# Attention in a two-layer hybrid trunk: score and value products of the two array halves issued in turns

## The chip, the cores and the metric

The kernel runs on one core of a Trainium2 chip. A core has a TensorE array of 128 rows by 128 columns for matrix products (PE in the profile; its weight loads are PEld), VectorE (DVE), ScalarE (ACT), GpSimd (POOL) and SyncE (SP), which here only starts DMAs. They work at the same time, each through its own queue of instructions in order, and wait for each other through semaphores. Operands lie in the on-chip memory SBUF; matrix products land in the accumulator memory PSUM. Data comes from the device memory by DMA.

The metric is the device time of one execution, in microseconds (us); less is better.

## The reference

The reference is two layers of a trunk on 256 tokens by 1024 channels. A layer mixes a gated delta rule (8 heads) with a sliding-window attention (16 query heads of 64 channels, 2 key and value heads, window 128, a learned sink for each head), projects both, merges them with gates, and ends in a gated feed-forward part. The change touches the attention alone. Its core:

```python
def swa_sink_attention(q, k, v, sinks):
    # q (B,T,16,64), k and v (B,T,2,64); blocks of 128 queries, each with its own block of keys and the one before
...
    s = jnp.einsum('bnqhgd,bnkhd->bnhgqk', qb, kb) * (D ** -0.5)
    rel = qi + SWA_BLOCK - kj
    mask = (rel >= 0) & (rel < WINDOW) & (blk * SWA_BLOCK + kj >= SWA_BLOCK)
    s = jnp.where(mask[None, :, None, None], s, -jnp.inf)
...
    m = jnp.maximum(jnp.max(s, axis=-1, keepdims=True), sink)
    p = jnp.exp(s - m)
    denom = jnp.sum(p, axis=-1, keepdims=True) + jnp.exp(sink - m)
    o = jnp.einsum('bnqhgk,bnkhd->bnqhgd', p / denom, vb)
```

The 256 tokens are two blocks of 128. The first block sees its own keys alone. A query of the second block sees the keys of its own block up to itself, and those of the first block that lie after its place: 128 keys in all, so one square of 128 by 128 holds all scores of a head, the upper triangle from the block before and the lower one from its own.

## The kernel before

**The time is that of the weights' products.** Every layer multiplies the normalized input with some 130 weight tiles. A weight tile comes by DMA on SP's queue into a pool of six buffers (`raw`, line 170), ScalarE rounds it to the TensorE's fast format (`wH`, L177), VectorE takes what the rounding lost (`wL`, L178), and TensorE adds three products for each block of 128 rows into the tile `acc`: rounded weights by rounded input (L193), by the input's rest (L194), rest of the weights by rounded input (L195). The pool also takes the tiles `wada` of the conditioning, which VectorE multiplies and sums (L231); a free buffer is what starts the next DMA.

**Order.** A scheduler puts the instructions of each engine in order by priority. The delta rule and attention are issued at a high priority (`chain()`), in the order of the list `CHAIN` (L28): in layer 0 "p s i 00 v 01 10 11", in layer 1 "p s i 00 10 01 11 v", where "p", "s", "i" and "v" are parts of the delta rule and two digits are one call `attention(tb, kv)`: the block of queries, and the key and value head. The gates' projections (`gate`, L192 to L195) fill TensorE between them. After the chain the projection of the attention's output (`sH`, `sL`; L956) is issued, which needs all four calls.

**One call of `attention`** works on the eight query heads of one key head. They lie in pairs: four pairs of heads, and in each pair the first head has its 64 channels on partitions 0 to 63 and the second on partitions 64 to 127 (`hfs`). So a score product (64 channels deep) uses one half of the array's rows: head 0 of a pair the upper, head 1 the lower. The four products of the first heads go into one PSUM tile, `ps_cur0`, those of the second heads into `ps_cur1` (L816), and in the second block of queries the products with the earlier keys into `ps_prv0` and `ps_prv1` (L825). The loops name the two halves in turns, but nothing holds the scheduler to that. The products are float32, and each is two instructions in the profile.

All these tiles, the transposes and the value products take their PSUM from one pool of two buffers (`pat`, L116): a tile waits until the last reader of the tile two before it is done.

Then each half `i` goes through the softmax by itself: in the first block L820 adds the mask; in the second L828 copies the scores on ScalarE and L829 puts the earlier keys' scores over them where the mask says so. L836 takes the maximum (VectorE), L845 the exponentials (ScalarE, four instructions), L851 scales by the reciprocal of the sum (ScalarE, four instructions), L854 transposes on TensorE into `ps_pT`. In the first block ScalarE copies the transposed probabilities to `pc` (L858) and one value product follows (L859). In the second VectorE writes two masked copies, `pc` and `pp` (L862, L863), and two value products follow (L864, L865), one with the values of each block. A value product has all 128 rows and 64 columns of the array: half 0 of the heads uses the first 64 columns and writes partitions 0 to 63 of the tile `ps_o`, half 1 the others. The value products of half 0 stand ahead of the transposes of half 1. At the end L867 rounds `ps_o` into `sH` on ScalarE, and L868 writes the rest, `sL`, on VectorE.

The SBUF tiles `s0`, `s1`, `pc` and `pp` share one tag of three buffers (`at2`, L304).

## Time and profile before

| what | value |
|---|---|
| timed runs, median of 3 | 1102.69 us (1102.17 to 1106.59) |
| the profiled execution's own time | 1078.32 us |
| its span (first to last instruction) | 1076.5 us |
| granted TensorE clock, mean | 0.997 |
| DMA, mean over the span | 196 GB/s |
| attention and what fills it, layer 0 | 195.5 to 298.1 us of the span |
| the same, layer 1 | 724.2 to 811.8 us |

The terms of the prediction are differences inside the span. The profiled execution lies 1.8 us above its span and 24.4 us below the median of the timed runs, so a difference is carried over to the median as it is. Rows of the trace are given by the line of the kernel that issued them; `x8` counts instructions, and "[0.78 <-DVE pc L862]" behind a row is the time for which the engine stood idle ahead of it, and who ended it.

### The profile page before, as it was taken

The page shows a single profiled execution, that of the slowest core. Times are in us where ns is not written, and L with a number is a line of the kernel's source. Part 1 is how long each engine was busy: PE and PEld are TensorE (multiplying, and loading weights), DVE is VectorE, ACT ScalarE, POOL GpSimd, SP SyncE. Part 2 cuts the span into 40 slices and gives each one's busy share as a digit, 9 for nine tenths or more (in the row PEclk, how much of TensorE's full clock was granted, in tenths as well). Part 3 has the DMA queues.
Part 4 walks back from the last instruction along what each step waited for, and adds up shares of the span by engine and source line. Part 5 has one row for each costly group of instructions (what it writes and reads, how often), then busy time and mean ns, then how long its engine had stood idle before and what let it go on. Part 6 is the DMA issues. An engine that isn't in the chain of part 4 may idle for free.

```text
span 1076.5 us, 23351 instructions
## 1 busy us (share of the span) xinstructions
PE 1038.8 (96%) x9248; PEld 985.9 (92%) x9248; DVE 846.0 (79%) x1891; ACT 648.3 (60%) x1325; POOL 4.0 (0%) x8
## 2 busy tenths in 40 slices
PE   3899989999999999999999999999999999999998
PEld 1799989978799999999999999997879999999998
DVE  6999976967768899988886999788456879777643
ACT  5388755677545675554445897658674457555432
POOL 0000000000000000000000000000000000000000
PEclk9999999999999999999999999999999999999999
DMA  9864565464555578888976545563015555555561
GB/s 361 323 204 156 193 239 168 154 209 138 170 203 178 175 235 290 284 271 274 333 267 188 174 156 199 196 198 117 23 58 179 193 178 177 179 186 179 179 202 36
DMA packets 60013, 210.48 MB, mean 196 GB/s; under 512 B 6784, under 2 KB 7808, under 8 KB 59904
## 3 DMA queue, kind: packets, MB, share of 16 engines
q1 hardware_dynamic: 59616, 208.72, 58.6%
q8 instruction: 72, 1.18, 0.4%
q10 hardware_dynamic: 288, 0.28, 0.1%
q14 instruction: 37, 0.30, 0.1%
HBM read 207.92 MB, written 1.05 MB: 194 GB/s over the span
## 4 chain that ended last, share of the span: by engine, by line
PE 79%; DVE 10%; ACT 6%; issue 3%; DMA 2%; SPq 0%; DVEq 0%; ACTq 0%
PE acc L193 21%; PE acc L195 21%; PE acc L194 21%; DVE wL L178 3%; ACT wH L177 2%; DVE early L231 2%; DMA raw<-wada 1%; PE ps_kk L607 1%; PE ps_cur L816 1%; PE pa L466 1%; PE pa L467 1%; PE pa L465 1%; DVE kq L553 1%; DVE raw L231 1%; PE ps_o L864 1%
## 5 line engine op out<-in xcount | busy, mean ns | idle before, releaser
L177 ACT CAST wH<-raw 128x1024 fp32r<-128x1024 f32 (+2 forms) x302 | 308.6, 1026 | 243.5 <-PE acc L194 193.8
L178 DVE TENSOR_TENSOR wL<-raw,wH 128x1024 fp32r<-128x1024 f32 (+2 forms) x302 | 360.2, 1195 | 90.9 <-ACT wH L177 87.6
L193 PE MATMUL acc<-hH,wH 128*128 128x256 f32 x1376 | 396.4, 288 | 0.0
L195 PE MATMUL acc<-hH,wL 128*128 128x256 f32 x1376 | 395.3, 287 | 0.1
L194 PE MATMUL acc<-hL,wH 128*128 128x256 f32 x1376 | 393.3, 286 | 0.0
L193 PEld LDWEIGHTS acc<-hH,wH 128*128 128x128 f32 x1376 | 264.1, 192 | 3.3 <-issue 1.8
L194 PEld LDWEIGHTS acc<-hL,wH 128*128 128x128 f32 x1376 | 263.9, 192 | 2.0 <-issue 1.6
L195 PEld LDWEIGHTS acc<-hH,wL 128*128 128x128 f32 x1376 | 263.9, 192 | 1.8 <-issue 0.8
L231 DVE SCALAR_TENSOR_TENSOR raw<-raw,cact 128x1024 f32<-128x1024 f32 x80 | 97.4, 1220 | 20.5 <-DMA raw<-wada 20.3
L195 PE MATMUL acc<-g_b,wL 128*128 128x256 f32 x224 | 63.5, 283 | 0.0
L193 PE MATMUL acc<-g_b,wH 128*128 128x256 f32 x224 | 63.5, 283 | 0.0
L194 PE MATMUL acc<-g_b,wH 128*128 128x256 f32 x224 | 63.4, 283 | 0.0
L553 DVE SCALAR_TENSOR_TENSOR kq<-cr,pt,kq 128x255 f32<-128x255 f32 (+2 forms) x96 | 45.7, 477 | 7.6 <-ACT kq L551 7.4
L193 PEld LDWEIGHTS acc<-g_b,wH 128*128 128x128 f32 x224 | 43.0, 192 | 0.0
L195 PEld LDWEIGHTS acc<-g_b,wL 128*128 128x128 f32 x224 | 42.9, 192 | 0.0
L194 PEld LDWEIGHTS acc<-g_b,wH 128*128 128x128 f32 x224 | 42.9, 191 | 0.0
L1015 DVE SCALAR_TENSOR_TENSOR g<-acc,pt,g 128x255 f32<-128x255 f32 x80 | 38.2, 478 | 0.9
L193 PE MATMUL acc<-sH,wH 128*128 128x256 f32 x128 | 36.2, 285 | 0.7 <-ACT sH L867 0.7
L194 PE MATMUL acc<-mL,wH 128*128 128x256 f32 x128 | 36.4, 285 | 0.0
L194 PE MATMUL acc<-sL,wH 128*128 128x256 f32 x128 | 36.2, 284 | 0.1
L195 PE MATMUL acc<-mH,wL 128*128 128x256 f32 x128 | 36.2, 283 | 0.0
L193 PE MATMUL acc<-mH,wH 128*128 128x256 f32 x128 | 36.2, 283 | 0.0
(335 smaller groups left out, 2004.3 us busy)
## 6 DMA issues: line engine op xcount, KB each, us to landing
raw<-wbig SPq DMA_DIRECT2D x232, 512.0 KB, 3.8
raw<-wada SPq DMA_DIRECT2D x80, 512.0 KB, 4.3
raw<-wdn SPq DMA_DIRECT2D x32, 512.0 KB, 4.2
raw<-wsa SPq DMA_DIRECT2D x24, 432.0 KB, 6.5
early<-wada SPq DMA_DIRECT2D x16, 512.0 KB, 9.1
raw<-wdn SPq DMA_DIRECT2D x16, 384.0 KB, 3.6
x<-xT SPq DMA_DIRECT2D x4, 256.0 KB, 5.5
out<-x SPq DMA_DIRECT2D x8, 128.0 KB, 2.5
```

Of the source, the lines that this page charges most:

```text
L177: A.copy(h, raw)
L178: V.tensor_tensor(lo, raw, h.bitcast(F32), ALU.subtract)
L193: PE.matmul(o, wh, ah, start=first, stop=False)
L194: PE.matmul(o, wh, al, start=False, stop=False)
L195: PE.matmul(o, wl, ah, start=False, stop=last)
L231: return V.scalar_tensor_tensor(raw, raw, 1.0, cact, op0=ALU.mult, op1=ALU.mult, accum_out=modp[l][:, f:f + 1])
L465: PE.matmul(o, hh[:, kt, sl], wh[:, k4], start=kt == 0, stop=False)
L466: PE.matmul(o, hh[:, kt, sl], wl[:, k4], start=False, stop=False)
L467: PE.matmul(o, hl[:, kt, sl], wh[:, k4], start=False, stop=kt == KT - 1)
L553: V.scalar_tensor_tensor(dst[:, sft:], cr[:, :T - sft], w_[:, 3 - sft:4 - sft], dst[:, sft:], op0=ALU.mult, op1=ALU.add)
L607: PE.matmul(pk_, t[:, 0, cs_], t[:, :, cs_], start=True, stop=True)
L1015: V.scalar_tensor_tensor(g[:, sft:], pa_[:, :T - sft], fw[:, i, 2 - sft:3 - sft], g[:, sft:], op0=ALU.mult, op1=ALU.add)
```

## The change

In the scores, a helper `scores` issues the eight products of a tile pair and ties each to the one before (`after`, which holds the order on the engine and adds no semaphore). So they stand in turns: first head, second head, of each pair. In the second block of queries the ScalarE copies of the current scores now stand ahead of the earlier keys' products in the program.

The transposed probabilities of both halves of the heads (`pc`, and `pp` in the second block) are kept until both are there. Then the value products are issued, again tied in turns: half 1, half 0 with the queries' own block, then, in the second block, half 1, half 0 with the earlier block. The PSUM tile `ps_o` is taken after the transposes of both halves and not before. The tag `at2` has six buffers in place of three. Each product, copy and mask is still made once.

```diff
--- before.py
+++ after.py
@@ -302,7 +302,7 @@
         return wk.tile([P] + list(shape), F32, name=name, tag="d2", bufs=3)
 
     def at2(name, shape=(4, P)):
-        return wk.tile([P] + list(shape), F32, name=name, tag="at2", bufs=3)
+        return wk.tile([P] + list(shape), F32, name=name, tag="at2", bufs=6)
 
     ssq = {}
 
@@ -808,27 +808,34 @@
             A.copy(kT[:, :, ts], pk)
 
         def attention(tb, kv):
+
+
             ts = slice(tb * P, tb * P + P)
             hfs = (slice(0, 64), slice(64, 128))
-            pcur = [pat([4, P], name=f"ps_cur{i}") for i in range(2)]
-            for j in range(4):
-                for i in range(2):
-                    PE.matmul(pcur[i][:, j], qT[hfs[i], kv * 4 + j, ts], kT[hfs[i], kv, ts], start=True, stop=True)
+
+            def scores(name, keys):
+                p2 = [pat([4, P], name=f"{name}{i}") for i in range(2)]
+                last = None
+                for j in range(4):
+                    for i in range(2):
+                        m = PE.matmul(p2[i][:, j], qT[hfs[i], kv * 4 + j, ts], kT[hfs[i], kv, keys],
+                                      start=True, stop=True)
+                        last = after(m, last) if last else m
+                return p2
+
+            pcur = scores("ps_cur", ts)
             s_ = [at2(f"s{i}") for i in range(2)]
             if tb == 0:
                 for i in range(2):
                     V.scalar_tensor_tensor(s_[i], bc(C("triu1"), 1, 4), NEG, pcur[i], op0=ALU.mult, op1=ALU.add)
             else:
-                pprv = [pat([4, P], name=f"ps_prv{i}") for i in range(2)]
-                for j in range(4):
-                    for i in range(2):
-                        PE.matmul(pprv[i][:, j], qT[hfs[i], kv * 4 + j, ts], kT[hfs[i], kv, 0:P],
-                                  start=True, stop=True)
                 for i in range(2):
                     A.copy(s_[i], pcur[i])
+                pprv = scores("ps_prv", slice(0, P))
+                for i in range(2):
                     V.copy_predicated(s_[i], bc(C("triu1"), 1, 4).bitcast(I32), pprv[i])
-            po = pat([4, P], name="ps_o")
             vs = slice(kv * 64, kv * 64 + 64)
+            pcs, pps = [], []
             for i in range(2):
                 s = s_[i]
                 hs = slice(kv * 8 + i, kv * 8 + 8, 2)
@@ -853,16 +860,21 @@
                 for j in range(4):
                     PE.transpose(pt_[:, j], s[:, j], C("ident"))
                 pc = at2("pc")
-                o = po[i * 64:i * 64 + 64]
+                pcs.append(pc)
                 if tb == 0:
                     A.copy(pc, pt_)
-                    PE.matmul(o, vtok[:, 0, vs], pc, start=True, stop=True)
                 else:
                     pp = at2("pp")
+                    pps.append(pp)
                     V.tensor_tensor(pc, pt_, bc(C("triu"), 1, 4), ALU.mult)
                     V.tensor_tensor(pp, pt_, bc(C("tril1"), 1, 4), ALU.mult)
-                    PE.matmul(o, vtok[:, 1, vs], pc, start=True, stop=False)
-                    tc.keep_in_program_order(PE.matmul(o, vtok[:, 0, vs], pp, start=False, stop=True))
+            po = pat([4, P], name="ps_o")
+            last = None
+            for blk, ops in ((tb, pcs),) if tb == 0 else ((1, pcs), (0, pps)):
+                for i in (1, 0):
+                    m = PE.matmul(po[i * 64:i * 64 + 64], vtok[:, blk, vs], ops[i], start=blk == tb,
+                                  stop=ops is pps or tb == 0)
+                    last = after(m, last) if last else m
             ks = slice(kv * 4, kv * 4 + 4)
             A.copy(sH[:, ks, ts], po)
             V.tensor_tensor(sL[:, ks, ts], po, sH[:, ks, ts].bitcast(F32), ALU.subtract)
```

The first place is on TensorE in layer 0, at the end of the call for block 0 and key head 0 and the start of the next one. Before, with `ps_pT_2914` the transposes of half 1, `pc_2892` and `pc_2919` the probabilities of half 0 and half 1, `acc` the filling projection and `ps_y16` a part of the delta rule:

```order
L859 MATMUL ps_o_2867<-pc_2892,vtok_185 64x512
L193 MATMUL acc_3486<-hH_182,wH_3376 128x256
L194 MATMUL acc_3486<-hL_183,wH_3376 128x256
L195 MATMUL acc_3486<-hH_182,wL_3377 128x256
L854 MATMUL ps_pT_2914<-ct_85,s1_2864 128x128 x4
L859 MATMUL ps_o_2867<-pc_2919,vtok_185 64x512
L816 MATMUL ps_cur0_3053<-kT_1104,qT_1103 128x128 x4
L661 MATMUL ps_y16_2632<-ut16_2630,lq_2540 32x32 x32
```

With the change (half 1 is `pc_2917`, half 0 `pc_2891`):

```order
L861 MATMUL ps_pT_2912<-ct_85,s1_2864 128x128 x4
L875 MATMUL ps_o_2919<-pc_2917,vtok_185 64x512
L875 MATMUL ps_o_2919<-pc_2891,vtok_185 64x512
L661 MATMUL ps_y16_2632<-ut16_2630,lq_2540 32x32 x32
L821 MATMUL ps_cur0_3053<-kT_1104,qT_1103 128x128
L193 MATMUL acc_3523<-hH_182,wH_3412 128x256
L194 MATMUL acc_3523<-hL_183,wH_3412 128x256
L195 MATMUL acc_3523<-hH_182,wL_3413 128x256
L193 MATMUL acc_3523<-hH_182,wH_3412 128x256
L667 MATMUL ps_z16_2667<-u32_2625,yt16_2665 32x32 x32
L821 MATMUL ps_cur1_3054<-kT_1104,qT_1103 128x128
L821 MATMUL ps_cur0_3053<-kT_1104,qT_1103 128x128
```

The value product of half 0 has moved behind the transposes of half 1 and stands beside that of half 1. Of the next call's scores the first now stands alone, since the first of `ps_cur1` needs the buffer of the value tile, and the others follow in turns; before, the four of `ps_cur0` stood together and those of `ps_cur1` came later.

The second place is on TensorE in layer 1, at the end of the last call. Before, from the value product of half 1 with its own block (`pc_10288`) to that with the earlier block (`pp_10289`); the `acc_10729` products belong to a gate (`hH`, `hL`):

```order
L864 MATMUL ps_o_10233<-pc_10288,vtok_7394 64x512
L193 MATMUL acc_10729<-hH_7230,wH_10628 128x256
L194 MATMUL acc_10729<-hL_7231,wH_10628 128x256
L195 MATMUL acc_10729<-hH_7230,wL_10629 128x256
L193 MATMUL acc_10729<-hH_7230,wH_10628 128x256
L194 MATMUL acc_10729<-hL_7231,wH_10628 128x256
L865 MATMUL ps_o_10233<-pp_10289,vtok_7394 64x512
L195 MATMUL acc_10729<-hH_7230,wL_10629 128x256
```

Behind these come 27 more products of the gates, and then the first of the `sH` projection. With the change:

```order
L861 MATMUL ps_pT_10280<-ct_85,s1_10218 128x128 x4
L875 MATMUL ps_o_10289<-pc_10285,vtok_7394 64x512
L875 MATMUL ps_o_10289<-pc_10257,vtok_7394 64x512
L875 MATMUL ps_o_10289<-pp_10286,vtok_7394 64x512
L875 MATMUL ps_o_10289<-pp_10258,vtok_7394 64x512
L193 MATMUL acc_10793<-sH_9633,wH_10693 128x256
L194 MATMUL acc_10793<-sL_9634,wH_10693 128x256
```

All four value products stand directly behind the transposes of half 1, and the projection of `sH` directly behind them; the gates' products stand further ahead in the call.

The third place is on VectorE in layer 0, in the last call, around the masks of half 0. Before (`raw` rows are the conditioning's products, `wL_3839` a weight tile, `pc_3264` and `pc_3294` half 0 and half 1):

```order
L862 TENSOR_TENSOR pc_3264<-ps_pT_3259,ct_85 128x512
L863 TENSOR_TENSOR pp_3265<-ps_pT_3259,ct_85 128x512
L848 TENSOR_TENSOR sme_3278<-sme_3278,es_3275 128x4
L849 RECIPROCAL sme_3278<-sme_3278 128x4
L231 SCALAR_TENSOR_TENSOR raw_4009,modp0_100<-raw_4009,cact_87 128x1024
L178 TENSOR_TENSOR wL_3839<-raw_3836,wH_3838 128x1024
L862 TENSOR_TENSOR pc_3294<-ps_pT_3289,ct_85 128x512
L863 TENSOR_TENSOR pp_3295<-ps_pT_3289,ct_85 128x512
```

With the change (`pc_3263` half 0, `pc_3291` half 1):

```order
L231 SCALAR_TENSOR_TENSOR raw_4009,modp0_100<-raw_4009,cact_87 128x1024
L869 TENSOR_TENSOR pc_3263<-ps_pT_3258,ct_85 128x512
L870 TENSOR_TENSOR pp_3264<-ps_pT_3258,ct_85 128x512
L855 TENSOR_TENSOR sme_3275<-sme_3275,es_3272 128x4
L856 RECIPROCAL sme_3275<-sme_3275 128x4
L869 TENSOR_TENSOR pc_3291<-ps_pT_3286,ct_85 128x512
L870 TENSOR_TENSOR pp_3292<-ps_pT_3286,ct_85 128x512
```

The conditioning's product `raw_4009` has moved ahead of the masks of half 0. The weight tile `wL_3839` stands ten rows ahead of it now, behind the maxima of the call, and the DMA that fills `raw_4009` takes the buffer that `wL_3839` frees.

## The prediction

> **What bounds the kernel now.** I read the page first: busy times, then the chain that ended last.
>
> ```profile
> span 1076.5 us, 23351 instructions
> PE 1038.8 (96%) x9248; PEld 985.9 (92%) x9248; DVE 846.0 (79%) x1891; ACT 648.3 (60%) x1325; POOL 4.0 (0%) x8
> PE 79%; DVE 10%; ACT 6%; issue 3%; DMA 2%; SPq 0%; DVEq 0%; ACTq 0%
> ```
>
> TensorE is busy for 96% of the span and carries 79% of the chain, so a microsecond of TensorE work that goes is a microsecond of time, as long as no other engine is late at that place. The next reading is therefore by stage: the windows of the eight attention calls, four of each layer (start:end; length, then busy time of PE, PEld, DVE, ACT and POOL, the clock, the DMA share and GB/s).
>
> ```profile
> 195.50:221.18 25.68, 23.66 (x161) 19.55 (x160) 23.52 (x97) 20.67 (x56) 0.00 (x0) 1.00 0.48 163
> 221.18:246.78 25.60, 25.28 (x478) 21.36 (x477) 14.96 (x35) 17.62 (x49) 0.00 (x0) 1.00 0.54 176
> 246.78:278.05 31.27, 31.20 (x230) 26.34 (x229) 26.24 (x68) 19.82 (x54) 0.00 (x0) 1.00 0.48 157
> 278.05:298.07 20.02, 17.79 (x112) 13.07 (x111) 13.85 (x32) 11.35 (x34) 0.00 (x0) 1.00 0.53 175
> 724.20:746.65 22.45, 19.99 (x138) 16.12 (x138) 21.82 (x97) 19.25 (x54) 0.00 (x0) 1.00 0.32 103
> 746.65:772.00 25.35, 25.07 (x466) 19.54 (x465) 11.61 (x28) 17.14 (x49) 0.00 (x0) 1.00 0.24 74
> 772.00:787.04 15.04, 14.95 (x106) 12.44 (x105) 7.53 (x24) 11.21 (x34) 0.00 (x0) 1.00 0.12 36
> 787.04:811.70 24.66, 24.66 (x179) 20.63 (x179) 15.67 (x37) 16.30 (x46) 0.00 (x0) 1.00 0.21 64
> ```
>
> Three kinds of call are seen. In the first of each layer TensorE stands idle for 2.0 and 2.5 us, while DVE and ACT are busy for over 80% of it: they set the pace. In the last of layer 0 TensorE is idle for 2.2 us. In the other five it is idle for 0.4 us or less: there a saved product shortens the call.
>
> **The scores.** How two halves of the rows stand beside each other is in the timeline of TensorE (start, busy time, line, count):
>
> ```profile
> 197.49 0.49 PE L816 MATMUL ps_cur<-kT,qT 64*128 64x128 f32 x4
> 197.91 0.39 PE L194 MATMUL acc<-hL,wH 128*128 128x256 f32 x1
> 246.78 1.16 PE L816 MATMUL ps_cur<-kT,qT 64*128 64x128 f32 x8
> 247.86 1.16 PE L726 MATMUL ps_KS<-s,kq 128*128 128x128 f32 x8
> 724.21 1.16 PE L816 MATMUL ps_cur<-kT,qT 64*128 64x128 f32 x16
> 725.30 0.39 PE L193 MATMUL acc<-hH,wH 128*128 128x256 f32 x1
> ```
>
> From start to next start, four products (8 instructions) of one half take 1.08 us (246.78 to 247.86); four of each half in turns (16 instructions) take 1.09 us (724.21 to 725.30): the second half costs nothing. One product of each half takes 0.42 us (197.49 to 197.91), so a run with k products of a half takes about 0.42 + (2k - 2) x 0.1115 us: 0.42, 0.64, 0.86, 1.09. By the order before, the scores stand in 20 runs, in all 22.8 us by these prices. The order after has 29 runs: 16 with one product of a half, 3 with two, 3 with three, 7 with four. That is 16 x 0.42 + 3 x 0.64 + 3 x 0.86 + 7 x 1.09 = 18.8 us. **Saved: 4.1 us.** It isn't half, since the second tile of scores waits for the buffer of the value tile before it, so the first score stands alone, and fillers come in between.
>
> **The value products.** Sums over the run (count | busy, mean ns | idle ahead; the 8 rounds of the earlier block's products, L865, are like those of L864), then TensorE's timeline of a lone one (two instructions), and of two that follow on the same columns:
>
> ```profile
> L859 PE MATMUL ps_o<-pc,vtok 128*64 128x512 f32 x16 | 8.6, 618 | 2.8 <-ACT pc L858 2.7
> L864 PE MATMUL ps_o<-pc,vtok 128*64 128x512 f32 x16 | 8.6, 618 | 1.3 <-DVE pc L862 1.3
> ...
> 216.26 1.07 PE L859 MATMUL ps_o<-pc,vtok 128*64 128x512 f32 x2
> 217.26 0.38 PE L193 MATMUL acc<-hH,wH 128*128 128x256 f32 x1
> ...
> 290.76 1.07 PE L864 MATMUL ps_o<-pc,vtok 128*64 128x512 f32 x2 [0.78 <-DVE pc L862]
> 291.67 1.02 PE L865 MATMUL ps_o<-pp,vtok 128*64 128x512 f32 x2
> 292.62 0.72 PE L854 MATMUL ps_pT<-ct,s 128*128 128x128 f32 x4
> ```
>
> A lone product holds TensorE for 1.00 us (216.26 to 217.26), two for 1.86 (290.76 to 292.62). The 24 products, 8 of each line (16 instructions), take some 23.8 us (8 x 1.00 for those of L859 and about 2 x 8 x 0.99 for the others, since many of those stand alone between fillers). If the two halves of the columns run beside each other as those of the rows do, the four calls of the first block need 1.00 us each, and the four of the second 1.86: 11.4 us. **Saved: 12.4 us.** If they run one after the other, it is 1.86 and 3.58 us: 4 x 0.86 + 4 x 1.72 = 10.3 us more. No row of before has two halves of the columns in turns. The nearest rows:
>
> ```profile
> 222.27 0.75 PE L661 MATMUL ps_y<-ut,lq 32*32 32x32 f32 x64
> 222.95 0.39 PE L193 MATMUL acc<-hH,wH 128*128 128x256 f32 x1
> ```
>
> 64 instructions on squares of 32 by 32 in 0.68 us are 11 ns each: tiles on other rows, and of other columns too, run together. That and the rows' halves make me take the full overlap, and keep the 10.3 us as the other bound. [...]
>
> **What is taken back.** The saved sum is 16.4 us. Where TensorE isn't the last to come, it becomes a wait. The value products of half 0 stood between the transposes of the halves and covered half 1's softmax; now nothing of theirs is there. Call by call:
>
> First calls of both layers: saved 1.0 us each (one value product), net 0.
>
> ```profile
> 217.89 1.20 PE L854 MATMUL ps_pT<-ct,s 128*128 128x128 f32 x4
> 220.18 1.07 PE L859 MATMUL ps_o<-pc,vtok 128*64 128x512 f32 x2 [1.09 <-ACT pc L858]
> ```
>
> The transposes come at the pace of ACT's scaling (1.20 us for four), and TensorE then waits 1.09 us for the copy. The product of half 0 at 216.26 lay ahead of that wait; without it TensorE only waits longer. So 2.0 us of the 16.4 are worth nothing.
>
> Layer 0, last call: the chain of waits there (start, length, what):
>
> ```profile
> 279.52 0.12 PE acc L194
> ...
> 279.78 1.05 ACT wH L177
> 280.86 1.24 DVE wL L178
> 282.11 4.50 DMA raw<-wada
> 286.64 1.23 DVE raw L231 x2
> 287.90 4.52 DMA raw<-wada
> ...
> 294.81 0.61 DVE pc L862
> 295.47 1.07 PE ps_o L864 x2
> ...
> 297.44 0.59 ACT sH L867
> ```
>
> The masks and maxima of that call, on VectorE, by their means over the run:
>
> ```profile
> L836 DVE TENSOR_REDUCE mx<-s 128x4 f32<-128x512 f32 x16 | 10.5, 675 | 0.1
> L829 DVE COPY_PREDICATED s<-ct,ps_prv 128x512 f32<-128x512 int32 x8 | 5.8, 733 | 1.0 <-PE ps_prv L825 1.0
> ```
>
> Two DMAs of 4.5 us, each started by a buffer that VectorE frees, hold up VectorE, and so the masks. TensorE saves 0.9 (scores) + 1.9 (values) = 2.8 us, but the order after puts `raw_4009` ahead of the masks of half 0, and its DMA waits for a `wL` behind the call's maxima. From the start of the call: scores in turns among fillers to 6.1 us; two masked copies and two maxima on VectorE 2.4 (0.6 each from start to start); the `wL` 1.2, so 9.7; DMA 4.5, to 14.2; its L231 1.1; two masks of half 0 1.2, to 16.5; reciprocal and scaling of half 1 1.4 (the 1.20 of row 217.89 and small steps); last transpose 0.2 and the mask 0.8, to 18.9; two pairs of value products 1.86 to 20.7; L867 and L868 0.7: 21.4, against 20.02 of the window. So this call gets 1.5 us longer, in place of 2.8 us shorter. If the DMA is started earlier than I think, the 2.8 us stay.
>
> Layer 0, second and third call: 0.7 (scores) + 1.0 (values) = 1.7, and 2.1 less 0.3 = 1.8 us. By the order after, more of VectorE's weight casts stand ahead of the second half's small steps; an estimate from one `wL` at 1.24 us (280.86), of which fillers cover about half, is 0.7 and 0.8 us back. Net 1.0 us each. Between nothing and the whole is possible here.
>
> Layer 1, second call: 1.4 + 2.1 = 3.5 us, no wait in the window to lose it to (DVE is busy 11.6 of 25.35 us): net 3.5. Third: 0.7 + 1.0, less the 0.7 of the second call of layer 0: net 1.0. Last: 0.8 + 2.0 = 2.8 saved. Before, TensorE has no gap at all in this window, because 28 gate products (28 x 0.12, as at 279.52, = 3.4 us) lie behind the last value product and cover ACT's L867. After, none is there, and the end of layer 0's last call shows what that looks like:
>
> ```profile
> 298.07 0.62 PE L193 MATMUL acc<-sH,wH 128*128 128x256 f32 x3 [0.68 <-ACT sH L867]
> ```
>
> Waits for the last transposes' scaling (about 1.1), for the mask (0.8, as at 290.76), and for `sH` (0.7), and some 0.8 of half 0's covering products: 3.4 us. Net -0.6.
>
> **The sum.** Layer 0: 0 + 1.0 + 1.0 - 1.5 = 0.5. Layer 1: 0 + 3.5 + 1.0 - 0.6 = 3.9. Together 4.4 us of the 16.4: the profiled execution would go from 1078.3 to 1073.9. The timed median lies 24.4 us above that execution; a difference in the span carries over, so 1102.7 - 4.4 = **1098.3 us**. The larger `at2` pool is costed at nothing: tiles of half 1 no longer wait for those of half 0, which no row above shows as a wait.
>
> **Rivals.** *Little is taken back.* If VectorE's queue in the second to last calls of layer 0 stays off the path, the 0.7, 0.8, 0.7 and 4.3 us come back less about 1.5: net some 9.4, 1093.3 us. For it: TensorE is what comes last in five of eight windows. Against it: in the last call of layer 0 the chain goes over DMA and VectorE, not TensorE.
>
> *Slower: the column halves run in series.* Then each of the 12 pairs costs 0.86 us more than in the sum, and all of it lies behind the transposes of half 1, on the chain, where half 0's products used to be cover: 4.4 - 10.3 = -5.9, 1108.6 us. It decides from 0.37 us for each pair on (4.4 / 12), that is if 43% of the second product isn't hidden. For it: the column halves share all 128 rows, through which both of them take different data, and no row shows such a pair. Against it: the 11 ns of the 32 by 32 squares.
>
> *The end stays where it is.* If in both layers what paces attention is ACT and VectorE with the DMAs behind them, the saved TensorE time all turns into waits, 1102.7 us. For it: the windows of the first calls. Against it: idle times of 0.4 us or less in five others.
>
> **How the numbers follow.** The waits swallow most: 0.47 (1098.3). Little is taken back: 0.22 (1093.3). In series: 0.25 (1108.6). The same end: 0.06 (1102.7). This kernel's measurement tells about 0.5%, 5.5 us, from no change, so the bounds are 1097.2 and 1108.2. Of the first case 0.14 lies below the lower one, and 0.01 above the upper one; of the second 0.19 below; of the third 0.18 above: faster 0.33, same 0.48, slower 0.19. The range leaves out a little less than half of the two outer cases: 1093.0 to 1109.0. The likeliest case by itself spans 1095.5 to 1101.
>
> **What would show it.** Within a pair of L875 the second product starts at once with the first where they run together, and 0.4 us or more behind it where not; a pair then takes 1.00 or 1.86 us to the next start. The scores' sum should fall by 4 us. In the first calls the wait for `pc` should be 2 us and no longer 1.1. In the last call of layer 0 the chain should show DMA, L231 and the mask in a row, and a window of some 21.5 us. In the last of layer 1, 0.7 us of waiting for `sH`. I am wrong if the windows of calls 2 and 3 don't get shorter, or if the pairs run in series.

## The result, and the profile after

The change made the kernel **slower by 1.2%**: the ratio of its time to that of before is 1.0116 (95% interval 1.0073 to 1.0159). The median of 20 runs is 1101.78 us, that of 20 runs of before 1086.97. (Here and below a ratio, and the clock and the time at full clock in the table of experiments, leave out runs more than 1.5% above the fastest of their kernel, among them one of this kernel at 1656.29 us and a mean clock of 0.558 whose cause isn't known; the table's last column has the means of all the others.) Before's runs go from 1075.8 to 1106.6 us, so the three of the start, with a median of 1102.69, lay at the upper end. The profiled execution after took 1102.19 us, before 1078.32: 23.9 us more.

From the page after: span, busy times, the PEclk row of the slices, and the chain by engine.

```profile
span 1100.4 us, 23348 instructions
PE 1047.0 (95%) x9248; PEld 995.6 (90%) x9248; DVE 846.1 (77%) x1891; ACT 647.8 (59%) x1325; POOL 4.0 (0%) x8
PEclk9999999999899999999999999899699999999999
PE 73%; DVE 11%; ACT 7%; DMA 4%; issue 4%; SPq 0%; ACTq 0%; DVEq 0%
```

VectorE and ScalarE are as busy as before, TensorE 8 us more although it has the same instructions. The new thing is PEclk: 8, 8 and 6 tenths in three slices, where the page before has 9 in all. The windows of the eight attention calls after (columns as in the prediction) show where:

```profile
193.14:218.53 25.39, 22.73 (x161) 19.36 (x160) 23.73 (x98) 21.01 (x58) 0.00 (x0) 1.00 0.50 160
218.53:244.94 26.41, 24.77 (x475) 21.49 (x475) 13.45 (x33) 16.69 (x49) 0.00 (x0) 0.94 0.46 156
244.94:279.12 34.18, 31.74 (x233) 27.89 (x231) 28.43 (x70) 20.23 (x55) 0.00 (x0) 0.95 0.47 158
279.12:301.90 22.78, 17.39 (x114) 12.33 (x112) 14.31 (x35) 11.55 (x34) 0.00 (x0) 0.85 0.52 174
736.74:760.13 23.39, 19.83 (x139) 16.04 (x138) 22.76 (x98) 19.60 (x55) 0.00 (x0) 0.96 0.34 113
760.13:795.82 35.69, 34.00 (x489) 29.34 (x487) 10.64 (x28) 18.13 (x50) 0.00 (x0) 0.69 0.10 30
795.82:813.87 18.05, 17.60 (x136) 15.08 (x134) 11.46 (x32) 13.45 (x40) 0.00 (x0) 1.00 0.32 96
813.87:836.84 22.97, 19.76 (x139) 14.95 (x137) 16.41 (x44) 14.29 (x44) 0.00 (x0) 0.93 0.30 94
```

Before, the granted clock was 1.00 in all eight. After, it is below 1.00 in six, and 0.69 in the second call of layer 1, which takes 35.7 us against 25.4. The value products did what was forecast (TensorE's timeline after):

```profile
277.26 1.08 PE L875 MATMUL ps_o<-pc,vtok 128*64 128x512 f32 x4
278.17 1.03 PE L875 MATMUL ps_o<-pp,vtok 128*64 128x512 f32 x4
279.12 0.48 PE L821 MATMUL ps_cur<-kT,qT 64*128 64x128 f32 x2
```

Four products, eight instructions, take 1.86 us from 277.26 to 279.12, as two did before: the column halves run fully side by side. But TensorE waits more. Its waits in layer 0's attention before (195.5 to 298.1 us), and after (193.1 to 301.9): total, times, longest.

```profile
PE ps_o L864 <- DVE pc L862: 1.3, 2, 0.8
PE ps_o L859 <- ACT pc L858: 1.1, 1, 1.1
...
PE ps_pT L854 <- ACT s L851: 0.4, 2, 0.2
...
```

```profile
PE ps_pT L861 <- ACT s L858: 5.4, 4, 2.3
PE acc L193 <- ACT gate L942: 2.0, 1, 2.0
PE ps_y L661 <- issue: 1.2, 1, 1.2
PE ps_o L875 <- ACT pc L865: 1.1, 1, 1.1
PE ps_o L875 <- DVE pc L869: 0.8, 1, 0.8
...
```

The transposes of half 1, which the value products of half 0 used to cover, now wait 1.2 to 2.3 us for ScalarE. (One wait of the first row, 1.62 us at 292.11, is that of half 0 in the last call.) Over all rows of this view TensorE waits 4.4 us in layer 0 before and 12.2 after; in layer 1 2.6 and 8.8. That is 14 us more. What such a wait does to the clock is seen in stretches of 3.41 us around two of them (windows after):

```profile
290.61:294.02 3.41, 1.21 (x4) 0.55 (x4) 2.04 (x6) 3.41 (x15) 0.00 (x0) 1.00 0.75 264
294.02:297.44 3.42, 1.35 (x4) 0.72 (x4) 1.44 (x5) 1.64 (x6) 0.00 (x0) 0.50 0.43 153
297.44:300.85 3.41, 3.10 (x8) 0.77 (x8) 2.16 (x5) 0.00 (x0) 0.00 (x0) 0.50 0.11 18
300.85:304.26 3.41, 2.61 (x18) 2.06 (x17) 0.69 (x1) 0.72 (x2) 0.00 (x0) 1.00 0.37 141
...
765.06:768.48 3.42, 2.27 (x135) 1.83 (x128) 0.00 (x0) 1.51 (x3) 0.00 (x0) 1.00 0.03 8
768.48:771.89 3.41, 3.41 (x32) 2.90 (x32) 0.83 (x3) 1.98 (x5) 0.00 (x0) 0.50 0.02 5
...
788.96:792.37 3.41, 3.41 (x32) 3.41 (x31) 1.54 (x4) 1.92 (x7) 0.00 (x0) 1.00 0.00 0
```

In this profile the clock is either 1.0 or 0.5, and every place at half clock starts a whole number of times 3.413 us behind the first (48.26 us), on one grid of stretches of 3.41 us. In 290.61 to 294.02 TensorE works 1.21 us: the next stretch, with 1.35 us of work, runs at half clock, and so does the one behind it, with 3.10. From 768.48 on the half clock lasts six stretches, 20.5 us. In all, the profiled execution after ran at half clock for 54.6 us, in nine places (41 us of it in the attention; its last 0.8 us are left out), and that of before for 6.8, in two. Half of the difference is 23.9 us, **as much as the two spans differ.** This counts every microsecond at half clock as half lost. By the line through many runs below (8.8 us for each 0.01 of mean clock, that is for 21.5 us at half clock) it is 0.41 of one, 19.6 us of the 23.9.

What stood in the stretch ahead of the nine places? In three (13.7 us of half clock) it was a wait of transposes for ScalarE. In three (30.7 us) it was a stop next to small products that the view puts down to "issue". In two (6.8 us) it was another wait, for a gate and for the feed-forward part. One, 48 us into the run, has its like before (at 50.5 us).

Two single executions are also a narrow base. In the profile of experiment e4, a kernel whose time is that of before, layer 1's second call loses the clock with none of the moved products (the columns are those of the windows above):

```profile
750.00:753.41 3.41, 2.15 (x7) 0.62 (x6) 3.24 (x12) 3.41 (x8) 0.00 (x0) 1.00 0.14 29
753.41:790.96 37.55, 37.55 (x450) 30.08 (x451) 11.38 (x27) 17.00 (x49) 0.00 (x0) 0.50 0.17 57
```

The stretch from 750.00 holds two waits of the first call, 0.17 us of the transposes and 1.08 us for `pc`. The profile of before has the same two, but there the grid parts them into two stretches, with 2.50 and 2.34 us of work (740.00 to 743.41 and on to 746.83), and the clock stayed. So the same two waits cost one run its clock and the other not, and what the change does to the clock is read from many runs.

### The profile page after: what moved, and what is told of

It reads as the page before. It is cut to its first block, busy times and chain, and to the rows that moved or that the text cites. A ratio compares the mean times of both kernels' runs of the same rounds, so it can differ in the third digit from the quotient of the medians.

```text
span 1100.4 us, 23348 instructions
## 1 busy us (share of the span) xinstructions
PE 1047.0 (95%) x9248; PEld 995.6 (90%) x9248; DVE 846.1 (77%) x1891; ACT 647.8 (59%) x1325; POOL 4.0 (0%) x8
## 4 chain that ended last, share of the span: by engine, by line
PE 73%; DVE 11%; ACT 7%; DMA 4%; issue 4%; SPq 0%; ACTq 0%; DVEq 0%
PE acc L193 19%; PE acc L194 19%; PE acc L195 19%; DMA raw<-wada 4%; DVE wL L178 4%; ACT wH L177 2%; DVE early L231 2%; PE ps_kk L607 1%; DVE raw L231 1%; PE ps_o L875 1%; ACT s L852 1%; PE pa L466 1%; PE pa L467 1%; PE pa L465 1%; PE ps_cur L821 1%
## 5 line engine op out<-in xcount | busy, mean ns | idle before, releaser
L194 PEld LDWEIGHTS acc<-hL,wH 128*128 128x128 f32 x1376 | 266.7, 194 | 3.4 <-issue 2.2
L195 PEld LDWEIGHTS acc<-hH,wL 128*128 128x128 f32 x1376 | 266.7, 194 | 1.1 <-issue 0.4
L231 DVE SCALAR_TENSOR_TENSOR raw<-raw,cact 128x1024 f32<-128x1024 f32 x80 | 97.6, 1222 | 20.3 <-DMA raw<-wada 20.2
L193 PE MATMUL acc<-g_a,wH 128*128 128x256 f32 x128 | 36.6, 286 | 0.0
L194 PE MATMUL acc<-g_a,wH 128*128 128x256 f32 x128 | 36.4, 284 | 0.0
L195 PE MATMUL acc<-g_a,wL 128*128 128x256 f32 x128 | 36.4, 284 | 0.0
```

The lines of the kernel that those rows point to most:

```text
L193: PE.matmul(o, wh, ah, start=first, stop=False)
L194: PE.matmul(o, wh, al, start=False, stop=False)
L195: PE.matmul(o, wl, ah, start=False, stop=last)
L231: return V.scalar_tensor_tensor(raw, raw, 1.0, cact, op0=ALU.mult, op1=ALU.mult, accum_out=modp[l][:, f:f + 1])
```

## The experiments

Three theories were put to the test. Theory 1: lost cover makes waits, and waits make half clock. Theory 2: products on two halves at once pull the clock down by themselves. Theory 3: the changed order of the other queues is what costs. The first results led to theory 1a, on scores next to small products.

The table is read by its last three columns. A straight line through 92 runs of before gives 1076.3 us at clock 1.000 and 8.8 us for each 0.01 of mean clock below it (correlation 0.95). "At full clock" is the mean time less 8.8 us for each 0.01; its standard error is 0.3 to 0.7 us, 1.2 and 1.5 for e5 and e8 with few runs. The clocks that the expectations from e6 on name are means of all runs, so they are held against the last column.

| kernel | ratio to before (95%) | mean clock | at full clock, us | all runs: mean us (clock) |
|---|---|---|---|---|
| before | 1 | 0.992 | 1076.3 | 1086.5 (0.989) |
| the whole change | 1.0116 (1.0073 to 1.0159) | 0.978 | 1076.7 | 1100.9 (0.972) |
| e1 scores only | 1.0115 (1.0058 to 1.0172) | 0.979 | 1079.9 | 1100.4 (0.977) |
| e2 values only | 1.0092 (1.0050 to 1.0134) | 0.974 | 1070.2 | 1098.4 (0.969) |
| e4 six buffers only | 0.9985 (0.9942 to 1.0027) | 0.992 | 1076.1 | 1088.9 (0.986) |
| e5 whole, waits filled | 0.9976 (0.9925 to 1.0027) | 0.990 | 1075.2 | 1089.9 (0.984) |
| e6 values, waits filled | 0.9977 (0.9929 to 1.0024) | 0.994 | 1073.2 | 1084.8 (0.987) |
| e7 whole, first calls' values undone | 1.0121 (1.0076 to 1.0166) | 0.976 | 1074.7 | 1101.1 (0.972) |
| e8 whole, last calls' values undone | 1.0113 (1.0060 to 1.0166) | 0.977 | 1076.2 | 1101.5 (0.973) |
| e9 values in the middle calls | 0.9951 (0.9907 to 0.9994) | 0.993 | 1072.8 | 1086.9 (0.984) |
| e11 scores, not next to squares | 1.0060 (1.0018 to 1.0102) | 0.987 | 1079.6 | 1093.2 (0.985) |
| e12 e9 and e11 together | 1.0062 (1.0015 to 1.0109) | 0.984 | 1076.1 | 1091.6 (0.982) |
| e14 whole, filled, e11's scores | 1.0063 (1.0019 to 1.0107) | 0.982 | 1075.4 | 1093.1 (0.980) |
| e15 scores, two places undone | 1.0096 (1.0053 to 1.0139) | 0.982 | 1079.2 | 1097.7 (0.979) |
| e16 scores, one place undone | 1.0100 (1.0062 to 1.0139) | 0.981 | 1079.5 | 1095.9 (0.981) |

### The parts by themselves: e1, e2, e4

e1 takes `scores` and the earlier copies from the change and leaves the rest as before; e2 takes the value products and the six buffers; e4 is one line:

```diff
-        return wk.tile([P] + list(shape), F32, name=name, tag="at2", bufs=3)
+        return wk.tile([P] + list(shape), F32, name=name, tag="at2", bufs=6)
```

> Scores tied in turns, value products and the three buffers as before. Theory 1 (the value products of half 0 were TensorE's work during half 1's softmax; without them its waits get longer, and a stretch of 3.4 us in which TensorE is idle for over 1.4 us is followed by at least one stretch at half clock): the cover is still there, so no more than the two half-clock stretches of before outside the attention; 0 to 4 us faster than before, ratio 0.996 to 1.000. Theory 2 (products on both halves of the array at once pull the clock down by themselves): half-clock stretches behind the score runs, ratio 1.003 to 1.006.

> Value products kept until both halves are there and issued in turns, six buffers; scores as before. Theory 1: the waits ahead of half 1's transposes and of the value products are as long as with the whole change (1.2 to 2.3 us in the first and last call of each layer), 4 to 6 half-clock stretches in the attention, ratio 1.010 to 1.018, so slightly slower than the whole change. Theory 2: much the same. Theory 3 (the scores' forced order pushes the filling products away): ratio 1.000 or below.

> Only the tag at2 with six buffers instead of three, all else as before. Theory 1: no effect, ratio 0.998 to 1.002, two half-clock stretches. Rival: more buffers let the scheduler reorder VectorE's and ScalarE's queues, and this is what costs; then ratio 1.005 or more.

The buffers do nothing to the time. The values alone came out slower as theory 1 said, though at 1.0092 just short of its range, with the lowest clock of all, 0.974; yet **at full clock they save 6.1 us**. Theory 3, by which they would have been no slower than before, does not hold for them. e2's waits in layer 0 are those of the whole change:

```profile
PE ps_pT L854 <- ACT s L851: 5.4, 4, 2.3
PE ps_o L868 <- ACT pc L858: 1.1, 1, 1.1
PE ps_o L868 <- DVE pc L862: 0.8, 1, 0.8
```

The scores alone were a miss: 1.0115 where at most 1.000 was expected, and 3.6 us more at full clock. e1's timeline in layer 1 shows a wait that theory 1 doesn't know:

```profile
746.10 0.75 PE L661 MATMUL ps_y<-ut,lq 32*32 32x32 f32 x64
...
747.54 0.75 PE L667 MATMUL ps_z<-u,yt 32*32 32x32 f32 x64
748.22 0.71 PE L821 MATMUL ps_cur<-kT,qT 64*128 64x128 f32 x6
751.26 1.01 PE L821 MATMUL ps_cur<-kT,qT 64*128 64x128 f32 x6 [2.33 <-issue]
```

In the middle of a run of scores TensorE stands for 2.33 us, and the view names nothing that it waits for ("issue"). Just ahead of it went two groups of squares of 32 by 32, 64 instructions in 0.75 us each. A half-clock stretch follows that lasts 27.3 us (750.3 to 777.6). Hence theory 1a: so many short instructions in so short a time that TensorE runs out of them.

### The waits filled: e5, e6

e5 is the whole change, with work for TensorE in the waits whose results are overwritten; e6 has the same lines on top of e2.

```diff
+                fill = (tb, kv) in ((0, 0), (1, 1))
+                if i and fill:
+                    for _ in range(3 + tb):
+                        after(PE.matmul(pt_[:, 0:2], C("ident"), x[:, 0], start=True, stop=True), turned)
...
+            for _ in range(2 if fill else 0):
+                after(PE.matmul(po[:, 0:2], C("ident"), x[:, 0], start=True, stop=True), turned)
```

> The whole change, and in the first and the last call of each layer idle work for TensorE: 3 or 4 products of 128x256 (0.45 us each, results overwritten) between the transposes of half 0 and half 1, and 2 ahead of the value products. In all 22 products, some 10 us of TensorE work, of which theory 1 says that most stands in waits. Theory 1: no half-clock stretch in the attention except by chance at one place, although the work is more: 5 to 12 us faster than the whole change, ratio to before 0.998 to 1.006. Theory 2: as many half-clock stretches as with the whole change (5 places or more), and 0 to 10 us slower than it.

> The value products in turns in all calls, scores as before, and in the first and last call of each layer the idle products of 128x256 ahead of half 1's transposes and ahead of the value products (22, some 10 us of TensorE work). Theory 1: neither the waits nor the stalls are there; clock 0.983 to 0.991 against 0.9685 of the value products without filling; ratio 0.993 to 1.000. Rival (the moved products cost by themselves): 1.007 or more.

**This is the test that decides.** With 22 more products, some 10 us of work that nobody uses, the kernel is 1.4% faster than without them (0.9976 against 1.0116). The clock goes from 0.978 to 0.990, and with the values alone from 0.974 to 0.994. Over all runs e5 gains 11.0 us on the change and stays 3.4 us above before; e6 gains 13.6 us on e2. In e5's profile the transposes wait 3.6 us for ScalarE, in that of after 9.6. At full clock e5 is no slower than the change, within its error, so its fillers stood in waits; e6 is 3.0 us slower than e2, so a third of them did not. The gain is the clock's. Theory 2 expected five or more places at half clock in the attention; the profile of e5 has one (20.5 us from 766.5 on, behind a stop next to small products), that of after six. So by these two profiles the fillers mend the lost cover, and the stops next to small products stay.

### Parts undone: e7, e8, e9

In each, `late` sets in which calls the value products are kept; in the others they stand as before, inside the loop over the halves.

```diff
+            late = (tb, kv) != (0, 0)                        # e7
+            late = (tb, kv) != (1, 1)                        # e8
+            late = (tb, kv) not in ((0, 0), (1, 1))          # e9, on top of e2
```

> The whole change, but in the first call of each layer (block 0, key head 0) the value products stand as before, half 0's ahead of half 1's transposes. Theory 1: the waits ahead of half 1's transposes there (1.2 and 1.8 us) go; the half-clock stretches near 225 us of layer 0 and, in layer 1, the one ahead of the small products of the delta rule's inverse, which lasts some 20 us, get rare. Ratio to before 1.002 to 1.008, mean clock 0.978 to 0.985 (whole change 0.972, before 0.989). Rival (the last calls or the scores alone carry the loss): 1.010 or more.

> The whole change, but in the last call of each layer (block 1, key head 1) the value products stand as before. Theory 1: the waits of 1.6, 2.3 and 2.1 us there go, and with them some 10 us of half clock, 5 us of time: ratio 1.005 to 1.010, mean clock 0.976 to 0.982. Rival: the first calls carry nothing, then this one comes down to 1.000.

> Scores as before; the value products kept and issued in turns only in the second and third call of each layer, which have fillers enough; first and last call as before. Theory 1: no new long waits, so the clock as before (0.987 to 0.991), and the products side by side save up to 1.0 + 2.1 us a layer: 2 to 6 us faster than before, ratio 0.994 to 0.999. Theory 2 (products of two halves side by side pull the clock down): ratio 1.004 or more.

e7 and e8 missed: undoing the first or the last calls alone brings the clock to 0.976 and 0.977 (over all runs 0.972 and 0.973), no better than the change. Why neither helps by itself stays open. Both together, without the scores in turns, are e9: clock 0.993, ratio 0.9951, and **3.5 us saved at full clock**, as much as was expected of it. Over all its twelve runs, though, the mean is 1086.9 us at clock 0.984, against 1084.5 at 0.991 for the 23 of before in that round. So the saving at full clock is shown; that e9 is faster as it runs, or keeps the clock of before, is not. Theory 2 is left to the next experiment.

### The clock by itself: m1

m1 has none of the reference in it: bursts of products of 128x256 with waits for ScalarE between them, then pairs on two halves, then squares.

> This kernel computes nothing of the reference; its output is the input. TensorE alone: bursts of 17 products of 128x256 (7.7 us) with a wait for ScalarE ahead of each, of eight lengths from 0.6 to 2.8 us, eight of each; then the two halves of the columns in turns (30 pairs) and in series (30 pairs), the two halves of the rows in turns, squares of 32 by 32 for 16 us, and the same behind a wait of 2.8 us. Theory 1: no half-clock stretch behind waits under 1.2 us, one behind each wait over 2.8 us that falls within one 3.4 us stretch, some between, by where the wait falls; none in the parts with two halves in turns. Pairs in turns 1.0 us, in series 1.86 us. Theory 2: half clock in the parts in turns, with no wait ahead. Behind the last wait the squares of 32 by 32 stay at half clock for several stretches, if the clock looks at how much of the array works and not at whether it works.

Two waits, each with the stretch of the grid that it falls in and the one behind (windows of m1: length, then PE, PEld, ACT and POOL, clock, DMA; no VectorE in it):

```profile
341.53:344.95 3.42, 1.43 (x7) 0.92 (x5) 1.92 (x2) 0.00 (x0) 1.00 0.00 0
344.95:348.36 3.41, 3.23 (x15) 2.87 (x16) 0.12 (x1) 0.00 (x0) 1.00 0.00 0
351.77:355.18 3.41, 1.39 (x7) 0.89 (x5) 1.95 (x2) 0.00 (x0) 1.00 0.00 0
355.18:358.59 3.41, 3.26 (x8) 2.64 (x9) 0.10 (x1) 0.00 (x0) 0.50 0.00 0
```

With 1.43 us of work in the stretch the clock stayed, with 1.39 it was halved for the next one. By the length of the wait, in m1: none of the 24 waits of 1.08, 1.42 and 1.67 us was followed by half clock, one of the eight of each of 1.92, 2.17 and 2.42 us, three of the eight of 2.75 and five of the eight of 3.25. As expected, none under 1.2 us did it, and of the longer ones some. Then the column halves in turns and in series, the rows' halves, and the first run of squares:

```profile
690.85:716.70 25.85, 25.85 (x121) 8.53 (x120) 0.00 (x0) 0.00 (x0) 1.00 0.00 1
729.90:781.50 51.60, 51.60 (x121) 16.36 (x120) 0.00 (x0) 0.00 (x0) 1.00 0.00 0
794.70:825.00 30.30, 30.30 (x401) 27.27 (x400) 0.00 (x0) 0.00 (x0) 1.00 0.01 2
838.15:880.60 42.45, 21.64 (x1537) 20.25 (x1536) 0.00 (x0) 0.00 (x0) 0.56 0.02 4
```

And TensorE's timeline at the start of the squares:

```profile
837.63 0.59 PE L120 MATMUL full<-x 128*128 128x256 f32 x2
838.15 1.82 PE L161 MATMUL sq<-x 32*32 32x32 f32 x187
842.34 1.49 PE L161 MATMUL sq<-x 32*32 32x32 f32 x128 [2.37 <-issue]
846.35 1.93 PE L161 MATMUL sq<-x 32*32 32x32 f32 x128 [2.51 <-issue]
```

Thirty pairs on two column halves take 25.85 us in turns against 51.60 in series, half as long, and the clock is 1.00 throughout, as with the rows' halves: theory 2 is gone. The first 187 squares take 1.82 us; then the timeline has 128 between one stop and the next, with no other engine at work. In the two runs of squares these are 22 stops, 40.3 us in all, the longest 2.5. TensorE is busy for 21.64 of the 42.45 us, and the mean clock there is 0.56.

What moves meanwhile is in the trace too. From 836 to 885 us one DMA queue alone moves data, that of the instructions (packets, MB, share):

```profile
q8 instruction: 12, 0.20, 1.7%
```

These are twelve packets for the 3072 instructions of the first run of squares (products and their weight loads): by division one packet for 256 of them, that is for 128 products, as many as stand between two stops. In the profiles of before and after the same queue moves 72 packets of 16,384 bytes for 18,496 products and weight loads, 257 for each. There are six stops of over 0.5 us that these two profiles put down to "issue", one in before and five in after; by the start and length of the packets in the trace, each ends 1.3 to 1.6 us after one of them is through. This fits theory 1a, that TensorE stands because its next instructions have not come; the times show no more than that.

### Where the scores cost: e11, e12, e14, e15, e16

```diff
+            near = (tb, kv) == ((0, 1), (1, 0))[l]           # e11, e12, e14
+            near = (l, tb, kv) == (0, 1, 1)                  # e16; e15 has both conditions
...
-                        last = after(m, last) if last else m
+                        last = after(m, last) if last and not near else m
```

> The scores alone in turns (values and buffers as before), but in the second call of each layer, whose scores stand among the delta rule's products of 32 by 32, the scores stand as before. Theory 1a (scores in turns take their instructions twice as fast; next to the 32 by 32 products, 64 of them in 0.7 us, TensorE's instructions run out, and the stall of 1 to 2.3 us trips the clock): no stall put down to issue in the attention of layer 1, mean clock back to 0.986 to 0.991, ratio 0.995 to 1.001. Rival (the forced order as such, or the earlier copy, costs): as with all scores in turns, 1.008 to 1.015.

> Both parts of the change where theory 1 says that they do no harm: scores in turns in all calls but the second of each layer, value products kept and in turns in the second and third call of each layer only. Theory 1: no stall for issue in the attention of layer 1, no new waits over 1.1 us; clock 0.984 to 0.991, ratio 0.991 to 0.998. Rival (it is the number of moved instructions, or the two halves side by side): 1.004 or more.

> The whole change, with both suspected causes taken away: idle products of 128x256 in the waits of the first and last call of each layer (22 of them, some 10 us of TensorE work), and in the second call of each layer, among the products of 32 by 32, the scores as before. Theory 1 with 1a: no stall for issue and no wait over 1.2 us in layer 1's attention; mean clock 0.986 to 0.991, at least that of the filling alone (0.984); ratio 0.992 to 0.999. If a third cause is left, ratio 1.003 or more and a clock under 0.982.

> Scores alone in turns, but as before in the second call of each layer and in the last call of layer 0. Theory 1a (stalls next to the 32 by 32 products) with 3 (in layer 0's last call the earlier scores shift VectorE's queue, so that the conditioning's DMA stands ahead of the masks and the transposes wait 1.7 to 3.9 us): both are gone, ratio 0.996 to 1.002, clock 0.985 to 0.991. If the scores in turns cost by themselves, 1.005 or more.

> Scores alone in turns, but as before in the last call of layer 0 alone. Theory 1a: the stall for issue among the scores of layer 1's second call is there (1 to 2.3 us), clock 0.978 to 0.985, ratio 1.004 to 1.010. Theory 3 alone (all of the scores' cost lies in layer 0's last call): ratio 0.996 to 1.002.

In e11, e12, e14 and e15 the ScalarE copies, too, stand as before in the calls left out.

The stall in layer 1's second call goes as expected: 2.3 us with e1 and 2.1 with e16, which have the scores in turns there, none with e11, e12 and e15, which don't. e16's ratio, 1.0100, is as theory 1a said, and theory 3 alone is out. But the other times missed. e11 came to 1.006 and not to 1.00, e12 to 1.0062, e15 with both places undone to 1.0096, and all four kernels with the scores alone lie 2.9 to 3.6 us above before at full clock. e14 still shows a stall of 1.6 us for issue among the squares themselves and came to 1.0063, which its expectation had kept for a third cause. Over all runs the clock of e11, e12, e14 and e15 is 0.979 to 0.985, under what was expected. And e11 and e15, with no such stall, lose the clock in layer 1's second call all the same (13.7 and 34.1 us in their profiles), behind the same two waits as in e4. So the stall behind the squares is real and half clock follows it (27.3 us in e1), but it isn't what the scores in turns cost at full clock. TensorE stands idle for 41.1 to 43.6 us in the profiles of these four kernels, against 37.7 in that of before and 36.6 in that of e4, so waits are part of it; in which of the other runs of scores they lie **stays open**.

## Why the prediction was wrong

It forecast 1098.3 us from 1102.7, a ratio of 0.996; measured is 1.0116. That the measured 1101.78 us lies within its 1093.0 to 1109.0 is luck: the three runs that it started from lay some 16 us above the median of twenty. By its steps:

- **Value products:** right. Four products on both halves take the 1.86 us forecast, and the values alone save 6.1 us at full clock. The rival that priced them in series, the only one on the slower side, is wrong. In m1 thirty pairs on two column halves take 25.85 us in turns against 51.60 in series. In the profile of after the load and the product of the second column half of a pair start 6 to 7 ns behind those of the first (243.93, 277.26 us).
- **Scores:** the products themselves were sized well: the profile of after has the 29 runs, in all 21.0 us from start to next start against 22.9 before, by an estimate some 19 without the half clock and one stop in them. But "saved: 4.1 us" is wrong as a term of the time: alone they cost some 3 us at full clock. By the two parts alone (-6.1 and +3.6) one would expect -2.5 for both; measured is +0.4, at errors of 0.5 to 0.7 each.
- **What is taken back:** right in place, too small. In layer 0's last call the chain is the one forecast, a `wL`, the DMA of `wada`, its L231, the masks:

```profile
287.79 1.14 DVE wL L178
288.92 0.03 DVE nm L846
288.95 3.37 DMA raw<-wada
292.32 0.02 issue
292.35 1.23 DVE raw L231 x2
293.58 0.60 DVE pc L869
```

  The call takes 22.8 us against 21.4 forecast, 6.8 of them at half clock. The sum gave back 12.0 us of the 16.4 saved. The new waits in the attention come to 14 us in the profile, and two of about 2 us each lie outside it, as much as was saved; at full clock nothing is left (1076.7 against 1076.3).
- **Its own signs** of being wrong came. The second and third calls got longer, not shorter: 26.4, 34.2, 35.7 and 18.1 us, against 25.6, 31.3, 25.4 and 15.0; three of the four have half clock in them, and all hold other filling products. In the first calls the wait for `pc` stayed at 1.1 us, where 2 us had been expected: the added wait, 1.2 and 1.8 us, stands ahead of the transposes of half 1. In layer 1's last call no wait for `sH` shows.
- **The step that failed** is the pricing of a wait at its own length. "A difference in the span carries over" holds only at one clock, and the sum took the clock of the quoted windows, 1.00, for granted. In the profile of after, waits of 1.2 to 2.3 us were followed by 3.4 or 6.8 us at half clock or, once next to the squares, by 20.5, where they left 1.21 to 2.27 us of work in one stretch. The prediction also left out the stops for issue, which came with the scores in turns next to the squares (before's profile has none in the attention). The half clock is nearly the whole loss: the mean clock fell from 0.992 to 0.978, at 8.8 us for each 0.01 some 12 us of the 12.6 between the means.
- The sign of it stood in the prediction, unread: the median of the timed runs lay 24.4 us above the profiled execution of the same kernel. By the line above, 1102.7 us is a mean clock of 0.970, against 0.997 in the profile.

In eight of the nine places of after, half clock followed 1.6 to 2.2 us of idleness within one stretch (work of 1.85 to 1.21 us), in the ninth, next to squares, 1.15 us (765.06); in e4 it followed 1.3 us (750.00).

## What to carry to other kernels

A TensorE wait is not paid at its length alone: where the profile shows the clock change, add up TensorE's work in the stretches in which it changes, here 3.41 us. In the profiles of before and after, from 20 us on, half clock followed every stretch at full clock that had 1.47 us of work or less, and some with up to 2.27 us, for 3.41 or 6.83 us or, once next to small products, 20.5. Before work is moved out of a wait, ask what stands there instead; work without any use can be worth more than the products saved (e5 is 1.4% faster than the whole change). And where one kernel's own runs differ by 3%, find out why before a change of 0.4% is added up.

## What the runs showed of the hardware that was not expected

- In the profiles of before and after every place at half clock starts on a grid of 3.41 us. Take from them the stretches at full clock from 20 us on without squares of 32 or 64. The eight with 1.47 us of work or less (1.47 at 47.09 in before, 1.00 to 1.46 in after) were all followed by half clock, those with more never (the lowest 2.02 at 36.85 in before, 2.21 at 212.10 in after). In e4 one with 2.15 us was (750.00). In m1 1.43 us kept the clock and 1.39 did not.
- With squares of 32 by 32 in it a stretch with 2.27 us of work, 135 instructions, was followed by half clock (765.06 in after), another with 2.23, 53 instructions, was not (215.52).
- In m1 the first 187 squares take 1.82 us; of the groups of 128 behind them one starts 4.0 us after the other (842.34 to 846.35), 2.51 us of it a stop. In e1 64 squares take 0.75 us. The queue of the instructions moved twelve packets for the 3072 instructions of that run of squares, and in before and after the six stops for issue of over 0.5 us ended 1.3 to 1.6 us behind a packet of 16,384 bytes.
